# A two-layer trunk on one core: layer 0's twice-used weights kept in parts, one more parked MLP unit, and five smaller edits

## The chip, the cores and the metric

The kernel runs on one core of a Trainium2 chip. The metric is the device time of one execution in microseconds (us). Before the change it is 2128.24 us, the median of three executions (2126.32 to 2133.12).

Five engines work side by side, each through its own instructions in order: TensorE (PE, its weight loads shown as PEld), VectorE (DVE), ScalarE (ACT), GpSimd (POOL) and SyncE (SP, which here only issues transfers). POOL issues transfers too. An engine whose next instruction waits holds everything behind it.

## The reference

A stream `x` of 1024 positions by 1024 features passes two layers. Layer 0 mixes positions with a gated linear recurrence (RG-LRU), layer 1 with forgetting attention (FoX); beside it, each layer has four heads of cross-attention into 256 memory tokens. Then come an output projection and an MLP.

```python
def reference(x, mem, norm_mix, norm_mem, w_mem_kv, xa_q_gain, xa_k_gain, w_out,
              norm_mlp, w_mlp_in, w_mlp_out, w_in_a, conv_w, conv_b, ...):
    for layer in range(DEPTH):
        h = rms_norm(x, norm_mix[layer])
        j = layer // N_MIXERS
        if layer % N_MIXERS == 0:
            y_mix, xq = rglru_group(h, w_in_a[j], conv_w[j], conv_b[j], ...)
        else:
            y_mix, xq = fox_group(h, w_in_b[j], b_forget[j], fox_q_gain[j], fox_k_gain[j])
        y_mem = memory_group(xq, mem, norm_mem[layer], w_mem_kv[layer], ...)
        x = x + jnp.concatenate([y_mix, y_mem], axis=-1) @ w_out[layer]
        x = x + sqrelu_mlp(rms_norm(x, norm_mlp[layer]), w_mlp_in[layer], w_mlp_out[layer])
    return x

def sqrelu_mlp(h, w1, w2):
    return jnp.square(jax.nn.relu(h @ w1)) @ w2
```

## The kernel before, in words

**Products in parts.** Every fp32 operand is held as two fp32r parts: `hi` is a rounded copy (ACT) and `lo` the rest (a DVE subtraction). A product of one 128x128 block with 512 columns is three matmuls: hi·hi, hi·lo, lo·hi. The two halves of the sequence (512 positions each) are worked on apart; `h` is the half.

**Weights.** A plan lists the weights in the order of use, each entry 128 x 1024 (for the output projections 128 x 512). SP loads the raw entry into a ring of three buffers `wr`; `_wpart` writes the parts into rings of three: `wh` by ACT (L312) and `wl` by DVE (L313). One full entry feeds 24 matmuls of 512 columns, a half entry 12. `share()` (L263) holds a list of weight names: an entry of a listed name is, at its first use, also stored to HBM in its two parts (`wsp`, two stores on SP's queue), and at a later use both parts are loaded from there (L328, two transfers on POOL's queue, straight into the rings), with no raw load and no work of ACT and DVE. Before the change the list holds only layer 1's weights. In layer 0 `wina` (8 entries), `wxqa` (4) and `wout0` (8) are used by half 0 and again by half 1, and are loaded raw and parted both times.

**Statistics of a norm.** The squares of 8 tiles of 512 positions are summed either by adds on DVE and POOL into one tile (`sqacc`, L440) which one small product reduces (L374), or on PE: `sq_pe`/`sq_mm` (L443 to L457) multiply each square (as weights) with a one-column vector, four matmuls of 128x1 per tile, 32 per half; each of these fp32 matmuls is two records of the trace. `norm_split_first` (L517) starts the program: it loads and parts half 0 of `x`, then takes the statistics with `sqacc`.

**The MLP.** For each of 8 units (`g`) `mlp_z` makes a block of the hidden layer for both halves and `mlp_out` multiplies it with the second weight, both by a scheme of seven products in place of eight, named b11, b21, t2, t3, t1, t4, b22. `t1` to `t4` are sums of the two halves' inputs, parted by ACT (L468) and DVE (L471). A product over a full entry is 24 matmuls (`product`, L1004). DVE adds a product to a tile in `plus` (L1027); `relu2` is L1031 (DVE) and L1032 (ACT). Partial sums go to HBM by accumulating transfers on POOL's queue (`xspill`, L1161). In the last unit (g = 7) the residual is added by transfers too: four per block, accumulating `xs` into the tile `dst` (L1180).

**Parked units.** The products b11 and b21 of a unit need only half 0. `mlp_park` runs them early, as PE work that fills gaps. TUNE["park"] = (0, 1): these two units' products run inside layer 1's FoX attention, which `weave` interleaves with the other work by a rate. TUNE["wait"] = (2,): this unit's two products run after the last output projection (`outproj(1, K_X)`), ahead of the MLP loop. When a parked unit comes up in `mlp_z`, its kept result is put back into PSUM by a matmul with the identity (L1092), and t2 accumulates onto it.

**FoX.** Per head: scores on PE (L1396, mask L1398), a maximum on DVE (L1401), exponentials on ACT (L246), a scaling on POOL (L1413), transposes on PE (L1438), copies of the result by ACT and DVE (L1441, L1442), and products with the values on PE (L1428, L1429).

**Order.** The code is written in program order with generators; a scheduler of the language, by its own model of times, then sets the order on each engine. Line numbers after the change are higher: L381 becomes L385, L440 L444, L456 L462, L1011 L1017, L1092 L1103, L1396 L1413, L1413 L1430, L1428 L1445, L1429 L1446, L1438 L1455, L328 L332, L852 L858, L863 L869.

## Time and profile before

| what | value |
|---|---|
| median of three executions | 2128.24 us (2126.32 to 2133.12) |
| the profiled execution | 2132.55 us |
| its span, first to last instruction | 2130.8 us |
| outside the span | 1.75 us |
| busy: PE, DVE, ACT, POOL | 97%, 78%, 53%, 40% |
| mean granted TensorE clock | 0.989 |
| moved over HBM | 295.29 MB, 139 GB/s |

How to read the views: a window row gives, for a stretch of the span, its length and for PE, PEld, DVE, ACT, POOL the busy time with the number of records, then the granted clock (1.00 is full), the share of time in which the 16 DMA engines were busy, and GB/s. A row of groups gives line, engine, operation, output and input tiles, shapes, count, busy us, mean ns, and the idle time of the engine just before such instructions. A row of the timeline gives start, length, and in brackets the idle time before and what ended it. Matmul records overlap and their ends are modelled, so PE can lose time while it counts as busy.

The stages in the profiled execution, roughly: 0 to 220 us half 0 of layer 0's input projections and the memory group, 220 to 320 the same for half 1 with the recurrence and the output projection, then layer 0's MLP to about 950, the inputs of layer 1 to 1110, FoX woven with projections and parked units to 1467, the last output projection to 1503, and layer 1's MLP to the end.

### The profile page before, as it was taken

To read this page: it belongs to the slowest core of one execution; us is meant where nothing else is said; L and a number is where in the kernel's file an instruction comes from. 1 tells how busy PE (TensorE), PEld (TensorE's weight loads), DVE (VectorE), ACT (ScalarE), POOL (GpSimd) and SP (SyncE) were. 2 spreads that over 40 slices of the span, in tenths; PEclk is the share of its full clock that TensorE was granted. 3 is DMA by queue.
4 is the path that set the end of the run, shared out by engine and by line. 5 is a ranking of instruction groups with operands and counts; after the bars stand their busy time and mean duration, and the time that the engine had idled before them with its cause. 6 is when DMAs were issued, how large, how long until landed. Compare 5 with 4: busy or idle time off the path is not lost.

```text
span 2130.8 us, 29902 instructions
## 1 busy us (share of the span) xinstructions
PE 2065.7 (97%) x10402; PEld 1716.9 (81%) x10402; DVE 1654.5 (78%) x2712; ACT 1137.0 (53%) x2154; POOL 857.8 (40%) x847
## 2 busy tenths in 40 slices
PE   8999999999999999988999999999989999999999
PEld 6798878778778778767998998877767777787787
DVE  8987688886876877887686778776877778768867
ACT  6765645544444444465555647565544444544443
POOL 3222221434535535545332324422063544444444
PEclk9999999999999999999999999998999999999999
DMA  6323352446446545647767446844255574374375
GB/s 208 119 80 109 114 188 85 95 88 135 98 91 128 103 94 121 132 114 199 278 239 269 148 135 218 294 137 127 93 113 126 118 150 92 76 158 86 80 171 139
DMA packets 124952, 295.29 MB, mean 139 GB/s; under 512 B 14016, under 2 KB 16128, under 8 KB 124800
## 3 DMA queue, kind: packets, MB, share of 16 engines
q1 hardware_dynamic: 79872, 203.11, 28.4%
q0 software_dynamic: 44928, 90.26, 23.8%
q8 instruction: 82, 1.34, 0.3%
q14 instruction: 70, 0.57, 0.1%
HBM read 185.22 MB, written 108.10 MB: 138 GB/s over the span
## 4 chain that ended last, share of the span: by engine, by line
PE 55%; DVE 13%; issue 6%; DMA 4%; ACT 1%; POOL 1%; DVEq 0%; SPq 0%; POOLq 0%; ACTq 0%
PE pspt L1011 15%; PE pss L1011 12%; PE pspj L381 10%; PE pspj L1011 8%; DVE wl L313 3%; DVE r L471 3%; DVE f L1031 2%; DMA xspill<-f 2%; PE pso L1011 2%; PE pspt L381 1%; PE pspt L1438 1%; PE pss L1396 1%; DMA f<-xspill 1%; DVE f L1027 1%; DVE f L1130 1%
## 5 line engine op out<-in xcount | busy, mean ns | idle before, releaser
L313 DVE TENSOR_TENSOR wl<-wr,wh 128x1024 fp32r<-128x1024 f32 (+2 forms) x362 | 442.2, 1232 | 112.6 <-ACT wh L312 108.0
L1011 PE MATMUL pspt<-r,wh 128*128 128x512 f32 x1552 | 490.2, 396 | 8.0 <-DVE f L1027 6.1
L1161 POOL DMA_DIRECT2D xspill<-f x224 | 292.3, 2029 | 299.0 <-DVE f L1027 296.7
L312 ACT ACTIVATE wh<-wr 128x1024 fp32r<-128x1024 f32 (+3 forms) x411 | 305.8, 766 | 149.7 <-PE pss L1011 36.3
L1011 PEld LDWEIGHTS pspt<-r,wh 128*128 128x128 f32 x1552 | 291.3, 188 | 79.9 <-ACT r L468 4.6
L1011 PE MATMUL pss<-r,wh 128*128 128x512 f32 x1024 | 329.9, 401 | 13.9 <-DVE r L471 5.1
L1011 PE MATMUL pspt<-r,wl 128*128 128x512 f32 x776 | 307.4, 396 | 0.4 <-DVE wl L313 0.2
L471 DVE TENSOR_TENSOR r<-f,r 128x512 fp32r<-128x512 f32 x282 | 225.0, 808 | 100.3 <-DMA xspill<-f 57.6
L1011 PE MATMUL pspj<-r,wh 128*128 128x512 f32 x816 | 259.3, 397 | 4.1 <-ACT f L1022 1.8
L381 PE MATMUL pspj<-wh,r 128*128 128x256 f32 (+1 forms) x1280 | 246.7, 286 | 3.9 <-ACT wh L312 1.7
L1011 PEld LDWEIGHTS pss<-r,wh 128*128 128x128 f32 x1024 | 193.2, 189 | 70.0 <-DVE r L471 12.8
L468 ACT ACTIVATE r<-f 128x512 fp32r<-128x512 f32 x282 | 172.8, 626 | 115.7 <-DMA xspill<-f 50.6
L1032 ACT ACTIVATE f<-f 128x512 f32<-128x512 f32 x128 | 80.9, 632 | 268.0 <-DVE f L1031 267.7
L381 PEld LDWEIGHTS pspj<-wh,r 128*128 128x128 f32 x1280 | 200.9, 188 | 7.0 <-ACT wh L312 1.9
L351 POOL TENSOR_TENSOR wr<-wr,wr 128x512 f32<-128x512 f32 x60 | 94.6, 1777 | 271.6 <-DVE wl L313 258.8
L1011 PE MATMUL pss<-r,wl 128*128 128x512 f32 x512 | 203.7, 398 | 0.0
L1011 PEld LDWEIGHTS pspj<-r,wh 128*128 128x128 f32 x816 | 153.0, 188 | 41.5 <-ACT f L1022 2.3
L381 PE MATMUL pspj<-wl,r 128*128 128x256 f32 (+1 forms) x640 | 181.5, 284 | 1.2 <-DVE wl L313 1.1
L1011 PEld LDWEIGHTS pspt<-r,wl 128*128 128x128 f32 x776 | 147.2, 190 | 37.3 <-DVE wl L313 2.1
L381 PE MATMUL pspj<-r,wh 128*128 128x512 f32 x488 | 163.7, 411 | 9.6 <-ACT wh L312 5.9
L1011 PE MATMUL pspj<-r,wl 128*128 128x512 f32 x408 | 160.0, 397 | 0.4 <-DVE wl L313 0.4
L353 POOL TENSOR_TENSOR wr<-wr,f 128x512 f32<-128x512 f32 x60 | 140.2, 2650 | 17.8 <-issue 17.6
(297 smaller groups left out, 4012.2 us busy)
## 6 DMA issues: line engine op xcount, KB each, us to landing
wr<-in_w_dram SPq DMA_DIRECT2D x134, 512.0 KB, 4.4
xspill<-f POOLq DMA_DIRECT2D x224, 256.0 KB, 6.8
f<-xspill SPq DMA_DIRECT2D x80, 256.0 KB, 3.9
xspill<-f SPq DMA_DIRECT2D x64, 256.0 KB, 3.8
f<-in_xT_dram SPq DMA_DIRECT2D x32, 256.0 KB, 3.4
wr<-in_wkv_dram SPq DMA_DIRECT2D x16, 512.0 KB, 4.0
wr<-in_wina_dram SPq DMA_DIRECT2D x15, 512.0 KB, 3.5
wsp<-wh SPq DMA_DIRECT2D x14, 512.0 KB, 4.7
```

The source lines that it names most:

```text
L312: self.wact = self.nc.scalar.activation(hi, raw, AF.Copy)
L313: eng.tensor_tensor(lo, raw, hi.bitcast(F32), ALU.subtract)
L351: G.tensor_tensor(r["a11"][:, d], r["a11"][:, d], r["a21"][:, d], ALU.subtract)
L353: G.tensor_tensor(r["a12"][:, d], r["a12"][:, d], x, ALU.subtract)
L381: self.lastmm = self.nc.tensor.matmul(out, lhsT=a, rhs=b, start=(j == 0), stop=(j == n - 1))
L468: i = self.nc.scalar.activation(hi[:, :n], src, AF.Copy)
L471: self.nc.vector.tensor_tensor(lo[:, :n], src, hi[:, :n].bitcast(F32), ALU.subtract)
L1011: self.lastmm = self.nc.tensor.matmul(ps, lhsT=a, rhs=b, start=(start and c == 0 and j == 0), stop=(c == n - 1 and j == 2), skip_group_che ...
L1027: self.nc.vector.tensor_tensor(f[:, :H], f[:, :H], ps, ALU.add)
L1031: self.nc.vector.scalar_tensor_tensor(f[:, n], src, 0.0, self.rsb[h][:, n], ALU.max, ALU.mult)
L1032: self.lastsq = self.nc.scalar.activation(f[:, n], f[:, n], AF.Square)
L1161: nc.gpsimd.dma_start(self.xs[2 * q + a, :, b * H:(b + 1) * H], f[:, n], accum_op=ALU.add)
```

## The change

1. Eight matmuls of 128 columns of ones are put at PE's start, before any data.
2. `wina`, `wxqa` and `wout0` join the list in `share()`: 20 entries of 512 KB per part are stored at first use (40 stores on SP) and loaded in parts at the second use (12 full entries of 2 x 512 KB and 16 half entries of 2 x 256 KB on POOL's queue).
3. `norm_split_first` uses `sq_pe`: eight adds (four on DVE) become 32 matmuls of 128x1, 64 records.
4. Unit 2 moves from "wait" to "park". Unit 3 becomes "wait": its b11 product runs before `outproj(1, K_X)`, its b21 after it.
5. For parked units other than 0, ACT copies the kept result into PSUM in place of the identity matmul.
6. In g = 7 of both layers, the block (0, 0) gets its residual by four POOL additions from tiles that SP loads at t1, in place of four accumulating transfers.

```diff
@@ TUNE
-    "park": (0, 1),
-    "wait": (2,),
+    "park": (0, 1, 2),
+    "wait": (3,),
@@ Builder.__init__
+        warm = self.psum("pt")
+        for _ in range(8):
+            nc.tensor.matmul(warm[:, :P], lhsT=self.ones, rhs=self.ones, start=True, stop=True)
@@ share
-            if len(e) < 5 or e[3][0] not in ('wkb','wqb','wvb0','wvb1','wxqb','wout1m','wout1x'):
+            if len(e) < 5 or e[3][0] not in ('wina','wxqa','wout0','wkb','wqb','wvb0','wvb1','wxqb','wout1m','wout1x'):
@@ sq_pe (and norm_split_first calls it)
-    def sq_pe(self, m, h, xt):
+    def sq_pe(self, m, h, xt, behind=None):
         sq = self.F.get()
-        self.nc.scalar.activation(sq[:, :H], xt, AF.Square)
+        i = self.nc.scalar.activation(sq[:, :H], xt, AF.Square)
+        if behind is not None:
+            self.after(i, behind)
...
-            self.sqacc(k, h, xt[k][:, :H], self.nc.vector if k % 2 else self.nc.gpsimd, last)
+            self.sq_pe(k, h, xt[k][:, :H], last)
@@ plan_mlp and the plan of layer 1
         for g in wait:
-            self.plan_unit("w1", 8 * l + g, Unit.ALL[:2])
+            self.plan_unit("w1", 8 * l + g, Unit.ALL[1:2])
...
+        for g in TUNE["wait"]:
+            self.plan_unit("w1", 8 + g, Unit.ALL[:1])
         self.plan += [self.ent("wout1x", m, 512, 1) for m in range(8)]
@@ mlp_park
         yield from self.product([self.psum("pj") for _ in range(2)], b11, True, self.copies(t))
         kept = []
+        if pause:
+            yield None
@@ mlp_z
-                nc.tensor.matmul(A[o], lhsT=self.ident, rhs=t[o][:, n], start=True, stop=True)
+                if g:
+                    nc.scalar.activation(A[o], t[o][:, n], AF.Copy)
+                else:
+                    nc.tensor.matmul(A[o], lhsT=self.ident, rhs=t[o][:, n], start=True, stop=True)
@@ mlp_out
-                if g == 7:
+                if g == 7 and a == b == 0:
+                    f = self.acc.pop(0)
+                    G.tensor_tensor(dst[q][:, n], dst[q][:, n], f[:, n], ALU.add)
+                    self.F.put(f)
+                elif g == 7:
                     nc.gpsimd.dma_start(dst[q][:, n], self.xs[2 * q + a, :, b * H:(b + 1) * H], accum_op=ALU.add)
@@ the end of the FoX stage
+        wait = [self.mlp_park(g, True) for g in TUNE["wait"]]
+        for p in wait:
+            while next(p) is not None:
+                pass
         drain(self.outproj(1, K_X, self.xs, self.xs, "gmlp1", True, ("pj", "s", "pt")))
         self.pool_parts = TUNE["pm1"]
-        self.mlp(1, TUNE["wait"])
+        self.mlp(1, wait)
```

The order on the engines moves at three places. First PE near the end of FoX, at the scores of one of the last heads (`pss` takes scores and, at L381, products of the output projection; `pso` the sums over values, `pspj` products of parked units). Before:

```order
L1396 MATMUL pss_14769<-r_1459_14148,r_1456_14134 128x512
L1396 MATMUL pss_14769<-r_1459_14148,r_1457_14135 128x512
L1398 MATMUL pss_14769<-msk,idr 128x128
L381 MATMUL pss_14986<-r_1356_13394,wh_73 128x512
L381 MATMUL pss_14986<-r_1357_13395,wh_73 128x512
L381 MATMUL pss_14986<-r_1356_13394,wl_76 128x512
```

After:

```order
L1413 MATMUL pss_14585<-r_1151_11370,r_1458_14194 128x512
L1413 MATMUL pss_14585<-r_1151_11370,r_1459_14195 128x512
L1017 MATMUL pspj_15060<-r_1503_14504,wh_73 128x512
L1017 MATMUL pspj_15060<-r_1504_14505,wh_73 128x512
L1017 MATMUL pspj_15060<-r_1503_14504,wl_76 128x512
L1017 MATMUL pspj_15060<-r_1515_14558,wh_73 128x512
L1445 MATMUL pso_14410<-r_1499_14476,r_1046_10501 128x512
L1017 MATMUL pspj_15060<-r_1516_14559,wh_73 128x512
L1017 MATMUL pspj_15060<-r_1515_14558,wl_76 128x512
L1017 MATMUL pspj_15060<-r_1521_14570,wh_73 128x512
L1017 MATMUL pspj_15060<-r_1522_14571,wh_73 128x512
L1446 MATMUL pso_14410<-r_1500_14477,r_1046_10501 128x512
```

The 72 matmuls of unit 2's two products and of unit 3's first (L1017) now stand between the rows of the attention's last heads; before, the only other work there was some of the output projection (L381).

Second, POOL in layer 0 during half 1's recurrence (L858 and L869 are scalar steps of the recurrence's scan, L444 adds of squares, the transfers are the new part loads of `wout0`). Before, POOL had these there, and no transfers:

```order
L852 TENSOR_SCALAR f_284_2866<-f_284_2866 128x512
L852 TENSOR_SCALAR f_283_2864<-f_283_2864 128x512
L440 TENSOR_TENSOR f_271_2797<-f_271_2797,f_293_2985 128x512
L863 TENSOR_SCALAR f_281_2860<-f_281_2860 128x512
L863 TENSOR_SCALAR f_282_2862<-f_282_2862 128x512
```

After:

```order
L869 TENSOR_SCALAR f_281_2926<-f_281_2926 128x512
L869 TENSOR_SCALAR f_282_2928<-f_282_2928 128x512
L332 DMA wh_74<-wsp_124 128x512
L332 DMA wl_77<-wsp_125 128x512
L869 TENSOR_SCALAR f_284_2932<-f_284_2932 128x512
L444 TENSOR_TENSOR f_271_2861<-f_271_2861,f_303_3111 128x512
L869 TENSOR_SCALAR f_283_2930<-f_283_2930 128x512
L332 DMA wh_73<-wsp_128 128x512
L332 DMA wl_76<-wsp_129 128x512
```

The loads of a part pair stand behind steps of the scan, which wait for DVE; two pairs (into buffers 74/77 and 73/76) are held that way, and the later ones follow one another.

Third, PE between the last output projection and the MLP of layer 1 (L456 and L462 are the norm's statistics). Before:

```order
L1011 MATMUL pspj_15254<-r_1514_14498,wh_74 128x512
L1011 MATMUL pspj_15254<-r_1515_14499,wh_74 128x512
L1011 MATMUL pspj_15254<-r_1514_14498,wl_77 128x512
L456 MATMUL pso_14978<-cD,f_1611_15172 128x1 x4
L456 MATMUL pso_14978<-cD,f_1614_15200 128x1 x4
L1011 MATMUL pss_15409<-r_1620_15221,wh_74 128x512
```

After:

```order
L1017 MATMUL pspt_15479<-r_1630_15398,wh_75 128x512
L462 MATMUL pso_15152<-cD,f_1626_15384 128x1 x4
L1017 MATMUL pspt_15478<-r_1631_15399,wh_75 128x512
L1017 MATMUL pspt_15478<-r_1630_15398,wl_78 128x512
L1017 MATMUL pspt_15479<-r_1631_15399,wh_75 128x512
L1017 MATMUL pspt_15479<-r_1630_15398,wl_78 128x512
L1017 MATMUL pss_15550<-r_1632_15405,wh_73 128x512
```

Before, a waiting unit's product stood ahead of the last statistics and t3 (`pss`) right behind them. Now t2 of unit 0 (`pspt`) stands ahead of them and four of its matmuls behind them, then t3.

More of the change, by code (lines that the diff above doesn't have):

```diff
@@ L86, in __init__ @@
         self.need = {n: () for n in names}
-        if "a11" in pos:
-            self.need["a11"], self.need["a12"] = ("a11",), ("a12",)
+        for k in ("a11", "a12"):
+            if k in pos:
+                self.need[k] = (k,)
         if full:
@@ L1013, in product @@
                 if c % 2 and c + 1 < n:
-                    yield
+                    yield 1
             if done is not None:
                 done(o, ps)
-            yield
+            yield 1
     def copies(self, dst):
@@ L1032, in relu2, with mlp_park @@
         self.lastsq = self.nc.scalar.activation(f[:, n], f[:, n], AF.Square)
-    def mlp_park(self, g):
+    def mlp_park(self, g, pause=False):
         t = []
@@ L1223, in hook7 @@
                 advance(nxt)
-        for g in wait:
+            if key == "t1":
+                self.acc = [self.load_x(2 * q, 0, self.xs) for q in range(4)]
+        for p in wait:
             for k in ("t3", "t1"):
                 self.xsplit(k)
-            drain(self.mlp_park(g))
+            drain(p)
         for g in range(8):
@@ L1668, in run @@
             self.R.put(v)
+        wait = [self.mlp_park(g, True) for g in TUNE["wait"]]
+        for p in wait:
+            while next(p) is not None:
+                pass
         drain(self.outproj(1, K_X, self.xs, self.xs, "gmlp1", True, ("pj", "s", "pt")))
         self.pool_parts = TUNE["pm1"]
-        self.mlp(1, TUNE["wait"])
+        self.mlp(1, wait)
 @with_exitstack
```

## The prediction

> **What bounds the kernel now.** I read the page first, then windows over the stages, then the waits and the timeline where a window loses time. The page:
>
> ```profile
> span 2130.8 us, 29902 instructions
> PE 2065.7 (97%) x10402; PEld 1716.9 (81%) x10402; DVE 1654.5 (78%) x2712; ACT 1137.0 (53%) x2154; POOL 857.8 (40%) x847
> ```
>
> PE is recorded busy for 97% of the span, so the kernel is bound by the count of matmuls plus the places where PE stands still or runs slowly. Work taken from DVE or ACT is worth something only at such a place. The windows, with the engines in the order of the header:
>
> ```profile
> core 0: us, PE busy (x) PEld busy (x) DVE busy (x) ACT busy (x) POOL busy (x), PEclk, DMA share, GB/s
> 5.40:13.60 8.20, 7.33 (x16) 4.95 (x17) 7.33 (x23) 6.88 (x13) 0.00 (x0) 1.00 1.02 367
> 30.60:34.10 3.50, 3.50 (x11) 2.87 (x11) 3.50 (x12) 0.00 (x0) 0.00 (x0) 0.51 0.33 112
> 280.00:400.00 120.00, 116.24 (x523) 93.22 (x522) 105.45 (x161) 68.83 (x112) 25.77 (x22) 0.99 0.42 125
> 286.65:290.06 3.41, 3.31 (x8) 2.63 (x9) 3.41 (x6) 2.26 (x5) 0.00 (x0) 0.50 1.00 368
> 1333.00:1361.00 28.00, 27.17 (x142) 22.19 (x141) 23.03 (x61) 16.11 (x41) 17.70 (x26) 1.00 1.04 352
> 1390.00:1467.00 77.00, 70.36 (x378) 55.65 (x378) 57.69 (x160) 50.30 (x121) 23.77 (x40) 1.00 0.36 103
> 1467.60:1481.30 13.70, 13.70 (x46) 11.44 (x46) 6.57 (x10) 5.25 (x9) 4.03 (x8) 0.50 0.68 212
> 1505.20:1512.00 6.80, 5.07 (x11) 3.57 (x12) 6.80 (x16) 2.52 (x4) 0.00 (x0) 0.50 0.01 2
> 1516.00:1590.00 74.00, 68.81 (x289) 53.56 (x288) 54.01 (x60) 34.62 (x56) 30.16 (x25) 1.00 0.38 102
> ```
>
> Two kinds of loss show: idle time (77.00 − 70.36 = 6.64 us in 1390 to 1467), and stretches at half the clock, which follow an idle time and cost half their busy time. The idle times that the change touches, from the timeline:
>
> ```profile
> 29.70 1.05 PE L374 MATMUL pso<-cD,f 128*128 128x1 f32 x8 [2.70 <-DVE f L440]
> 286.75 0.80 PE L924 MATMUL pspt<-r,wl 128*128 128x512 f32 x1 [2.46 <-DVE wl L313]
> 951.62 0.77 PE L1011 MATMUL pspt<-r,wh 128*128 128x512 f32 x1 [4.18 <-DVE f L1027]
> 1506.15 1.22 PE L1011 MATMUL pss<-r,wh 128*128 128x512 f32 x2 [2.35 <-ACT r L468]
> 1508.15 0.79 PE L1011 MATMUL pss<-r,wh 128*128 128x512 f32 x1 [0.79 <-DVE r L471]
> ```
>
> The pace of PE where nothing holds it, for scale, is this piece of the chain that ended last: 24 matmuls of 512 columns, one product, in 5.58 us, 0.233 each.
>
> ```profile
> 1592.02 5.58 PE pspt L1011 x24
> ```
>
> The profiled execution took 2132.55 us, its span plus 1.75 outside it, and is 4.31 above the median of the runs, 2128.24. I sum against the profiled one and give the difference on the median. About 0.3%, 6.4 us, is what a measurement here can tell from no change.
>
> **Part by part.**
>
> Warm-up matmuls. They have no input to wait for and stand before the first data. PE's first product waits for loads: in 5.40 to 13.60 the DMA engines are busy all the time (1.02), and 16 records there take 7.33 us where 16 × 0.233 would take 3.73. If the pace there were set by the clock, up to 7.33 − 3.73 = 3.6 us would be won. I take 0: PE then stands idle again until the first loads land, and 2.46 us of idle before 286.75 were enough to bring the half clock of 286.65 to 290.06. Range −3.6 to 0.
>
> Statistics on PE at the start. The price of one record is from the same operation further on, 16 in 1.84 us:
>
> ```profile
> 1501.96 1.84 PE L456 MATMUL pso<-cD,f 128*128 128x1 f32 x16
> ```
>
> 64 records × 0.115 = +7.4. The eight records at 29.70 go (−1.05), with their wait (−2.70) and the half clock behind it (3.50 × 0.5 = −1.75). That is +1.9, of which PE's idle time in 5.40 to 13.60 (8.20 − 7.33 = 0.87) can hold some: I take **+1**. Range: −5.5 if all of the new records lie beside waits for loads, +6.4 if none does and the idle time only moves. What the adds free on DVE is no gain, since PE isn't waiting for DVE elsewhere in that stage.
>
> Layer 0's second half in parts. The work that goes from DVE and ACT, by these groups of 280 to 400:
>
> ```profile
> L313 DVE TENSOR_TENSOR wl<-wr,wh 128x1024 fp32r<-128x1024 f32 x10 | 12.2, 1223 | 3.5 <-ACT wh L312 3.4
> L312 ACT ACTIVATE wh<-wr 128x1024 fp32r<-128x1024 f32 x10 | 10.6, 1056 | 6.3 <-PE pspt L1011 2.7 <-PE pspj L1011 2.6 <-DMA wr<-in_w_dram 0.9
> L313 DVE TENSOR_TENSOR wl<-wr,wh 128x512 fp32r<-128x512 f32 x14 | 9.6, 682 | 0.3 <-ACT wh L312 0.3
> ```
>
> DVE loses 12 × 1.22 + 16 × 0.68 = 25.5 us of work, ACT 12 × 1.06 and the half entries. Almost all of it lies beside PE's work; the one wait that it makes is 286.75, where `wl` stood behind the scan on DVE: −2.46, and the half clock 3.31 × 0.5 = −1.7, together −4.2. What comes instead is the latency of the part loads. For layer 1's entries, which already go this way:
>
> ```profile
> L328 POOL DMA_DIRECT2D wh<-wsp x32: 527/548/647, 1151.7 to 1483.9; - x32
> DMA to landing us min/median/max: 2.6/5.3/9.6
> wh<-wsp POOLq DMA_DIRECT2D x16, 256.0 KB, 3.9
> wl<-wsp POOLq DMA_DIRECT2D x16, 256.0 KB, 4.8
> ```
>
> A half entry feeds 12 matmuls, 12 × 0.233 = 2.8 us. In a ring of three the period is the larger of 2.8 and (L + 2.8)/3, L from the buffer's release to the landing; it stays 2.8 up to L = 5.6. The 256 KB loads took 3.9 and 4.8 (mean 4.35), so the steady run is covered by the two other buffers. Two pairs can't be issued early, since POOL stands at steps of the scan before them; with one buffer's work as cover each shows 4.35 − 2.8 = 1.55, together +3. Sum **−1.2**, range −4.2 to +8. The 20 MB of stores go out in the first half; SP's later raw loads stand behind them, but a store waits for the same subtraction that frees the raw buffer.
>
> Layer junction, g = 7. The four accumulating transfers become POOL additions. A POOL addition took
>
> ```profile
> L351 POOL TENSOR_TENSOR wr<-wr,wr 128x512 f32<-128x512 f32 x60 | 94.6, 1777 | 271.6 <-DVE wl L313 258.8
> 949.67 1.21 DVE L313 TENSOR_TENSOR wl<-wr,wh 128x1024 fp32r<-128x1024 f32 x1
> 950.80 0.67 DVE L1027 TENSOR_TENSOR f<-f,pspt 128x512 f32<-128x512 f32 x1
> ```
>
> 1.78 us, against a transfer of some us. The wait of 4.18 at 951.62 ended with the DVE addition of 950.80, which stood behind the weight subtraction of 949.67; in the new order the addition comes ahead of it. So −1.2, with the POOL additions free where POOL has time (40% busy). But POOL's additions slow DVE:
>
> ```profile
> L1031 DVE SCALAR_TENSOR_TENSOR f<-f,f 128x512 f32<-128x512 f32 x6 | 8.0, 1352 | 0.0
> L1031 DVE SCALAR_TENSOR_TENSOR f<-f,f 128x512 f32<-128x512 f32 x4 | 2.7, 684 | 0.0
> ```
>
> The same operation took 1352 ns on average in 280 to 400 and 684 in 1390 to 1467. I take 0.2 for that: **−1**, range −5 (the whole wait and more) to +3 (four DVE operations at +0.67).
> [...]
>
> FoX tail. Three products more, 3 × 5.58 = 16.8 us of PE work, now stand among the last heads' rows, and leave the MLP stage. In 1390 to 1467 PE was idle for 6.64; the waits are short and many, which is what a filler covers. DVE is 57.69 of 77.00 busy, 75%; the three products add to it three weight subtractions and four operations of 512, 3 × 1.22 + 4 × 0.68 = 6.4 us, and about as much to ACT. I take the whole idle and nothing of the time in which a busy PE loses pace: **−6.6**. Range 0 (each filler is paid for by DVE and ACT being later) to −6.64 − 6.85 = −13.5, if the half clock of 1467.60 to 1481.30 (13.70 × 0.5) goes as well.
> [...]
>
> After the last output projection. Before, 3.14 us of idle (2.35 + 0.79) stood between the statistics and t3, and a half clock with 5.07 × 0.5 = 2.5. Now t2 of unit 0 is there as filler, but only four of its matmuls (0.93 us) stand behind the last statistics: t3's parts are late by DVE and ACT as before. I take 0.93 of the idle and some 1.1 of the clock: **−2**. Range −5.6 (all) to +5.2 (the idle of 1516 to 1590, 74.00 − 68.81, once more, because unit 2's products no longer lie there).
>
> Identity matmuls.
>
> ```profile
> 1484.26 1.72 PE pspt L1092 x4
> L1441 ACT ACTIVATE r<-pspt 128x512 fp32r<-128x512 f32 x22 | 12.2, 592 | 4.6 <-PE pso L1428 2.4 <-PE pspt L1438 2.0
> ```
>
> Each record took 0.43 on PE; units 1, 2 and now 3 need none, so eight of twelve go: **−3.4**. ACT copies six tiles, 0.59 each by the row of L1441, 53% busy. If t2 had to wait for each pair, it would be 3 × 1.2 = 3.5 us, and the term 0.
>
> Sum: 0 + 1 − 1.2 − 1 − 6.6 − 2 − 3.4 = −13.2, so 2119.35 for an execution like the profiled one, and 2128.24 − 13.2 = **2115.0** on the median. The ends of the terms are extremes. As independent errors they give the root of the squares, 12 below and 15 above; two thirds of it is my forecast's own range, 2107 to 2125.
>
> **Rivals.**
>
> *All gaps filled.* The filler also removes the half clock at 1467.60 and all of the idle after the output projection: the FoX term −13.5 and the next −5.6, together −13.2 − 6.9 − 3.6 = −23.7, 2104.5; with a warm-up that works 2101. For it: DVE is only 75% busy in the tail, POOL 31%. Against: the half clock began at the end of the tail, behind a chain of the last head that no earlier filler shortens.
>
> *The tail is a chain of latencies.* Scores, maximum, exponentials, transposes and copies of the last heads set the end; three products' DVE and ACT work lengthens it as much as PE gains, and t3 waits as before. FoX and the next term are 0: −13.2 + 6.6 + 2 = −4.6, 2123.6, within 0.3%. For it: the order has t3 right behind the statistics still. That the warm-up does nothing belongs here as in my forecast.
>
> *Part loads late (slower).* In layer 0 the loads share the DMA engines with SP's loads and are issued by POOL behind the scan. At L = 9.6, the longest landing of the row, the half entries' period is (9.6 + 2.8)/3 = 4.13, 16 × 1.33 = 21.3 more, and the two pairs show 2 × 6.8 = 13.6: the term is −4.2 + 34.9 = +30.7, and the total −13.2 + 31.9 = +18.7, 2146.9. It decides from L = 7.0 on (7.33 × L − 35.5 = 13.2 + 3), and by 0.3% from L = 7.9. For it: such landings exist, in 1333 to 1361, where the DMA share is 1.04. Against: in 280 to 400 the share is 0.42, and loads of 512 KB in place of 256 KB of raw add less than as much again.
>
> **How the numbers follow.** My forecast 0.5, all gaps filled 0.18, the chain of latencies 0.2, part loads late 0.12. Below 2121.8 (faster by over 0.3%) lie nearly all of the first (0.47), all of the second and a quarter of the third (0.05): 0.70. Above 2134.6 lies most of the last (0.10) and little else (0.01): 0.11. Between: 0.19. The range goes from 2099, under the best case by the same two thirds of its unknown terms, to 2131, above the chain of latencies with its statistics term at the upper end; outside it stay most of the late loads and a few per cent below.
>
> **What would show it.** In the new trace: (1) no idle time at 29.70 and 64 more records of 128x1 before 45 us; (2) no wait for `wl` near 286, and waits of layer 0's second half for `wh<-wsp` and `wl<-wsp` of under 5 us in all; (3) in the last 77 us of FoX an idle time of PE under 2 us, and the stage itself longer by about 10 (16.8 − 6.6), with MLP shorter by 16.8; (4) behind the last statistics about 2 us of idle before t3; (5) four records of the identity matmul. Landings over 7 us in 220 to 400, or an FoX stage longer by the full 16.8, would make it wrong; so would waits of t2 for ACT's copies.

## The result

The changed kernel takes 2149.21 us (median of four runs, 2146.76 to 2152.37), beside 2129.47 of the kernel before on the same chip: a ratio of 1.0090, 95% interval 1.0073 to 1.0106. It is slower by 19 us where I forecast a gain of 13. The profiled execution took 2148.11 us, 15.6 more than the one of before, so the profile shows most of the loss.

The page of the changed kernel, its first two lines:

```profile
span 2146.4 us, 30066 instructions
PE 2077.2 (97%) x10466; PEld 1733.0 (81%) x10466; DVE 1628.6 (76%) x2668; ACT 1122.7 (52%) x2120; POOL 885.2 (41%) x900
```

PE is busy for 97% as before, with 64 records more: 64 of statistics and 16 of warm-up come, 8 of the old statistics and 8 of identity matmuls go. DVE has 26 us less to do (1654.5 to 1628.6), as the sum had it, and the kernel is slower all the same. Where the time went is read from the MLP's accumulating transfers, 112 per layer, whose line has its first and last start in a row (L1161 before, L1172 after):

```profile
L1161 POOL DMA_DIRECT2D xspill<-f x224: 846/1690/4885, 391.4 to 2055.5; - x112
```

```profile
L1172 POOL DMA_DIRECT2D xspill<-f x224: 853/1718/4912, 399.5 to 2066.8; - x112
```

The first is 8.1 us later, the last 11.3, and the end of the span 15.6: half of the loss is made before layer 0's MLP, 3.2 between there and the last transfer of layer 1, 4.3 in the last unit. Each of these positions is of one execution. Four kernels that share the code up to the first of these transfers (this one, and those without part 6, without part 4 and with the later fetch below) have it at 399.5, 399.6, 403.2 and 401.1, so a shift of under 4 us in one pair of profiles shows nothing by itself. The windows of the changed kernel that answer to those of before:

```profile
core 0: us, PE busy (x) PEld busy (x) DVE busy (x) ACT busy (x) POOL busy (x), PEclk, DMA share, GB/s
13.25:23.49 10.24, 10.24 (x62) 8.91 (x61) 7.41 (x22) 8.88 (x16) 0.00 (x0) 1.00 1.04 405
23.49:37.15 13.66, 13.66 (x50) 12.21 (x50) 11.06 (x28) 7.45 (x18) 4.51 (x4) 0.50 0.88 343
132.72:136.13 3.41, 3.03 (x14) 3.03 (x15) 2.64 (x14) 0.34 (x2) 1.85 (x5) 0.50 0.18 65
1390.00:1467.00 77.00, 74.91 (x390) 61.95 (x389) 58.21 (x150) 50.16 (x111) 20.68 (x35) 0.98 0.47 151
1733.57:1740.40 6.83, 6.08 (x14) 4.79 (x15) 5.13 (x5) 6.73 (x12) 2.96 (x2) 0.50 0.14 19
2112.45:2115.86 3.41, 3.36 (x9) 2.15 (x8) 3.41 (x5) 1.81 (x4) 1.37 (x1) 0.50 0.00 0
```

The half clock stands out. The row of before for the start had 3.50 us at 0.51; now it is 13.66 us at 0.50, and PE never stands still in them. The mean clock of the execution falls from 0.989 to 0.983:

```profile
core 0: 2146.4 us, clock 0.983
```

The windows of all stretches at half clock, added up, before (six stretches) and after (twelve):

```profile
sum 44.37, PE 38.99 PEld 31.92 DVE 36.90 ACT 22.13 POOL 13.23; mean PE 6.50 PEld 5.32 DVE 6.15 ACT 3.69 POOL 2.21
```

```profile
sum 75.10, PE 65.59 PEld 54.05 DVE 63.71 ACT 43.26 POOL 30.62; mean PE 5.47 PEld 4.50 DVE 5.31 ACT 3.60 POOL 2.55
```

PE is busy for 26.6 us more at half pace, which is 13.3 us of work lost. Of the 15.6 us that the span grew, 11.5 are busy time of PE (2065.7 to 2077.2) and 4.1 idle time (65.1 to 69.2), so the slower pace is about the size of the first part. So the theories to test were what brings each of these stretches, and which waits stand ahead of them. Three waits of the changed kernel, from its timeline:

```profile
133.10 0.58 PE L385 MATMUL pspj<-wh,r 128*128 128x256 f32 x1 [4.03 <-DMA wh<-wsp]
1734.32 1.22 PE L1017 MATMUL pss<-r,wh 128*128 128x512 f32 x2 [2.91 <-ACT f L1028]
2111.78 0.50 PE L1017 MATMUL pss<-r,wh 128*128 128x512 f32 x1 [3.05 <-DVE r L477]
```

The first belongs to part 2 (a part load), the second to part 4 (unit 2 in the MLP), the third to part 6 (POOL's additions in the last unit).

### The profile page after: what moved, and what is told of

Same layout as the page of the kernel before. It is cut to its first block, busy times and chain, and to the rows that moved or that the text cites. A ratio compares the mean times of both kernels' runs of the same rounds, so it can differ in the third digit from the quotient of the medians.

```text
span 2146.4 us, 30066 instructions
## 1 busy us (share of the span) xinstructions
PE 2077.2 (97%) x10466; PEld 1733.0 (81%) x10466; DVE 1628.6 (76%) x2668; ACT 1122.7 (52%) x2120; POOL 885.2 (41%) x900
## 4 chain that ended last, share of the span: by engine, by line
PE 35%; DVE 8%; DMA 4%; issue 4%; ACT 2%; POOL 1%; SPq 0%; DVEq 0%; POOLq 0%; ACTq 0%
PE pspj L385 9%; PE pspt L1017 7%; PE pss L1017 6%; PE pspj L1017 5%; DVE r L477 2%; DVE wl L317 1%; DMA xspill<-f 1%; DMA f<-xspill 1%; PE pss L1413 1%; DVE f L1037 1%; PE pspt L385 1%; PE pspt L1455 1%; DMA f<-cscr 1%; PE pso L1017 1%; DVE f L1033 1%
## 5 line engine op out<-in xcount | busy, mean ns | idle before, releaser
L1017 PE MATMUL pspt<-r,wh 128*128 128x512 f32 x1536 | 485.2, 396 | 8.1 <-DVE r L477 2.6
L317 DVE TENSOR_TENSOR wl<-wr,wh 128x1024 fp32r<-128x1024 f32 (+3 forms) x322 | 400.2, 1252 | 117.6 <-ACT wh L316 111.9
L1172 POOL DMA_DIRECT2D xspill<-f x224 | 292.5, 2097 | 286.8 <-DVE f L1033 283.4
L316 ACT ACTIVATE wh<-wr 128x1024 fp32r<-128x1024 f32 (+3 forms) x371 | 282.0, 782 | 151.3 <-DMA wr<-in_w_dram 45.5
L1017 PE MATMUL pss<-r,wh 128*128 128x512 f32 x1024 | 333.9, 404 | 23.2 <-ACT f L1028 12.0
L1017 PEld LDWEIGHTS pspt<-r,wh 128*128 128x128 f32 x1536 | 288.0, 188 | 79.5 <-DVE r L477 4.2
L477 DVE TENSOR_TENSOR r<-f,r 128x512 fp32r<-128x512 f32 x282 | 235.7, 847 | 100.8 <-ACT r L474 47.8
L1017 PE MATMUL pspt<-r,wl 128*128 128x512 f32 x768 | 304.8, 397 | 0.5 <-DVE wl L317 0.4
L1017 PE MATMUL pspj<-r,wh 128*128 128x512 f32 x832 | 265.7, 400 | 2.1 <-DVE f L1033 1.0
L1017 PEld LDWEIGHTS pss<-r,wh 128*128 128x128 f32 x1024 | 194.4, 191 | 80.8 <-DVE r L477 14.2
L1017 PE MATMUL pss<-r,wl 128*128 128x512 f32 x512 | 204.9, 401 | 0.0
L1017 PEld LDWEIGHTS pspj<-r,wh 128*128 128x128 f32 x832 | 156.6, 190 | 39.4 <-ACT f L1028 1.3
L1017 PEld LDWEIGHTS pspt<-r,wl 128*128 128x128 f32 x768 | 145.7, 190 | 36.8 <-DVE wl L317 2.2
L385 PE MATMUL pspj<-r,wh 128*128 128x512 f32 x488 | 164.4, 410 | 6.4 <-ACT r L474 2.1
L1017 PE MATMUL pspj<-r,wl 128*128 128x512 f32 x416 | 162.8, 397 | 0.0
```

Of the source, the lines that this page charges most:

```text
L316: self.wact = self.nc.scalar.activation(hi, raw, AF.Copy)
L317: eng.tensor_tensor(lo, raw, hi.bitcast(F32), ALU.subtract)
L385: self.lastmm = self.nc.tensor.matmul(out, lhsT=a, rhs=b, start=(j == 0), stop=(j == n - 1))
L477: self.nc.vector.tensor_tensor(lo[:, :n], src, hi[:, :n].bitcast(F32), ALU.subtract)
L1017: self.lastmm = self.nc.tensor.matmul(ps, lhsT=a, rhs=b, start=(start and c == 0 and j == 0), stop=(c == n - 1 and j == 2), skip_group_che ...
L1172: nc.gpsimd.dma_start(self.xs[2 * q + a, :, b * H:(b + 1) * H], f[:, n], accum_op=ALU.add)
```

## The experiments

Theory A: the loss is a sum of such waits and half clocks, one or two for each of parts 2, 3, 4 and 6. Its first rival, B: late part loads in layer 0 carry it alone, as my slower case had it. C and D deny A's reading of parts 4 and 3; E and F, later, are on what brings the half clock. Ratios are to the kernel before on the same chip in the same runs; the changed kernel stands at 1.0090.

**Part 6 undone.**

```diff
-                if g == 7 and a == b == 0:
-                    f = self.acc.pop(0)
-                    G.tensor_tensor(dst[q][:, n], dst[q][:, n], f[:, n], ALU.add)
-                    self.F.put(f)
-                elif g == 7:
+                if g == 7:
...
-            if key == "t1":
-                self.acc = [self.load_x(2 * q, 0, self.xs) for q in range(4)]
```

> The changed kernel with part 6 undone: the residual of block (0, 0) comes by four accumulating transfers again. Theory A (the loss is a sum of small terms; POOL's additions block DVE): in the changed kernel's last unit three POOL additions of 5.09 us stand beside three DVE operations of 1.77 in place of 0.68, then PE waits 3.05 us and runs at half clock; so the last unit is shorter by about 4 us and the junction of the layers by 2 to 3: about -6.5 against the changed kernel, +13 against the kernel before. Theory B (late part loads in layer 0 alone): no difference, +19 against the kernel before.

Measured: 1.0036 (1.0023 to 1.0049), −0.54%. In the profile the first accumulating transfer is as late as with the change and the end of the span 7.8 earlier: 3.3 by the last transfer of layer 1, 4.5 in the last unit. The mechanism is in the changed kernel's timeline, POOL first, then DVE:

```profile
2105.49 5.09 POOL L1192 TENSOR_TENSOR f<-f,f 128x512 f32<-128x512 f32 x3 [2.99 <-ACT f L1028]
```

```profile
2105.38 0.68 DVE L1147 TENSOR_TENSOR f<-f,f 128x512 f32<-128x512 f32 x1
2105.98 1.77 DVE L477 TENSOR_TENSOR r<-f,r 128x512 fp32r<-128x512 f32 x1
2107.68 1.77 DVE L1138 TENSOR_TENSOR f<-f,f 128x512 f32<-128x512 f32 x1
2109.38 1.75 DVE L1149 TENSOR_TENSOR f<-f,f 128x512 f32<-128x512 f32 x1
2111.05 1.28 DVE L477 TENSOR_TENSOR r<-f,r 128x512 fp32r<-128x512 f32 x2
```

From 2105.49 to 2110.6 POOL adds, and in just this time three DVE operations take 1.77 us in place of 0.68: 3.3 us late. The fourth, behind them, is what PE waits for at 2111.78, and the half clock of 3.41 follows. Without part 6 the waits of that stretch are gone:

```profile
PE pss L1017 <- ACT r L474: 0.7, 1, 0.7
```

At the junction of the layers the changed kernel shows the same, POOL first:

```profile
947.10 6.30 POOL L1192 TENSOR_TENSOR f<-f,f 128x512 f32<-128x512 f32 x4 [0.70 <-ACT f L1028]
948.83 1.75 DVE L477 TENSOR_TENSOR r<-f,r 128x512 fp32r<-128x512 f32 x1
950.63 0.50 PE L1017 MATMUL pspt<-r,wh 128*128 128x512 f32 x1 [2.57 <-DVE r L477]
956.47 1.22 PE L1017 MATMUL pss<-r,wh 128*128 128x512 f32 x2 [2.29 <-ACT r L474]
```

Three DVE operations in a row, from 948.83 to 953.9, take 1.75 to 1.77 us. Without part 6 the two waits are 0.48 and 0.49, but the old one of 4.18 is back at 4.17, where the change has 2.08. Layer 0's last spill store (L1177) starts at 1007.0 with the change and at 1003.6 without part 6, 3.4 earlier.

Theory A's mechanism holds, with a size of 0.54% against its 0.3. The undoing also takes out SP's four loads at t1 and their tiles, so the time is that of the part as a whole; that DVE's slowness beside POOL carries it is read from the two timelines. Theory B, no difference, falls: the intervals do not meet.

**Part 4 undone.** Park (0, 1), wait (2), with the plan and the calls as before the change.

```diff
-    "park": (0, 1, 2),
-    "wait": (3,),
+    "park": (0, 1),
+    "wait": (2,),
```

> The changed kernel with part 4 undone: units 0 and 1 are parked in FoX, unit 2 waits until after the last output projection. Theory A (a third unit fetched from HBM costs tiles): the waits of t2's bank for ACT's copies at the end of the b21 product of mlp_out for units 1 and 2 (3.03 and 2.91 us, each with a half clock behind it) are smaller, -9, but the filling of FoX (+4 us of use) is lost: about -5 against the changed kernel. Theory C (the filler is what helps and the stalls come from elsewhere): +4 against the changed kernel. Theory B: no difference.

Measured: 1.0064 (1.0044 to 1.0085), −0.26%. It points to theory A, and theory C's +4 lies outside; but the interval overlaps the changed kernel's (1.0073 to 1.0106), so that part 4 costs anything is not shown by this run alone.

**Part 2 undone.**

```diff
-'wina','wxqa','wout0','wkb','wqb',
+'wkb','wqb',
```

> The changed kernel with part 2 undone: layer 0's second uses are loaded raw and parted by ACT and DVE again. Theory A: the wait of 4.03 us for a part load at 133 us and its half clock go, the one behind the scan's DVE work stays: -3 to -6 against the changed kernel. Theory B (late part loads carry the whole loss): -18 or so, level with the kernel before or better.

Measured: 1.0008 (0.9995 to 1.0021), −0.82%: by the time it is what theory B expects, which part 6 has already ruled out as the whole. Nor does its profile put the loss in layer 0 alone:

```profile
L1172 POOL DMA_DIRECT2D xspill<-f x224: 845/1662/4865, 393.7 to 2056.0; - x112
```

The first transfer is 5.8 us earlier than with the change, the last 10.8. In the first 400 us no wait above 1.3 us is left: the one at 133 is gone, and so is one of 3.34 at 281. The rest is in layer 1. From 1500 to 1800 PE's waits for ACT's copies (L1028) are 8.2 us in place of 12.0, and the half clock from 1510 to 1800 is 3.4 us in place of 17.1. This can't be put down to part 2 as it stands: with the sums by 512-column matmuls, an edit at the start (below), the same waits fall to 7.0.

**Part 3 undone.**

```diff
-            self.sq_pe(k, h, xt[k][:, :H], last)
+            self.sqacc(k, h, xt[k][:, :H], self.nc.vector if k % 2 else self.nc.gpsimd, last)
```

> The changed kernel with part 3 undone: the first norm's squares are added on DVE and POOL again. Theory A: 64 records at 0.11 us go, of which the old wait of 2.7 us and its half clock come back: -2 to -4 against the changed kernel. Theory D (statistics on PE hide in the time in which PE waits for loads): +2 to +4. Theory B: no difference.

Measured: 1.0065 (1.0042 to 1.0088), −0.25%. Theory D's +2 to +4 lies outside the interval; that of theory A overlaps the changed kernel's, as with part 4. The same stretches as above:

```profile
13.25:23.49 10.24, 10.24 (x41) 8.18 (x41) 9.93 (x24) 7.84 (x14) 2.60 (x3) 0.90 1.03 388
23.49:37.15 13.66, 13.66 (x75) 11.67 (x74) 13.47 (x27) 9.82 (x24) 7.84 (x4) 1.00 0.93 352
```

The second has the full clock; the 0.90 of the first is the end of another half clock, from 8.50 to 15.33. The end of this profile is no earlier (2146.5), since other half clocks stand in it at 93.83, 145.03 and 278.15. All six profiles with `sq_pe` at the start have 13.65 us at half clock, one of them 17.07, from 22 to 25 us on; none without it has.

**Part loads on SP.**

```diff
-                    nc.gpsimd.dma_start(b, d[:, a:a + n])
+                    (nc.sync if k[0] in ('wina', 'wxqa', 'wout0') else nc.gpsimd).dma_start(b.bitcast(F32), d[:, a:a + n].bitcast(F32))
```

> The changed kernel with layer 0's part loads issued by SP in place of POOL. Theory A1 (the loads at 126 us are late because POOL issues them behind the scan's last step, which waits for DVE): the wait of 4.03 us at 133 us and its half clock go, so that layer 0 ends about 5 us earlier: -4 to -6 against the changed kernel. Theory A2 (the loads are late because the transfers themselves are slow beside the stores): the wait stays, 0 against the changed kernel.

Measured: 1.0052 (1.0034 to 1.0071), −0.38%; the wait is down to 0.80, at 130.86, with no half clock behind it, and the first accumulating transfer is 4.6 earlier:

```profile
L1172 POOL DMA_DIRECT2D xspill<-f x224: 842/1694/4880, 394.9 to 2061.9; - x112
```

Theory A1. POOL's timeline of the changed kernel shows how it came:

```profile
120.02 1.46 POOL L869 TENSOR_SCALAR f<-f 128x512 f32<-128x512 f32 x1 [3.97 <-DVE f L868]
124.75 1.47 POOL L869 TENSOR_SCALAR f<-f 128x512 f32<-128x512 f32 x1 [3.28 <-DVE f L868]
126.17 0.56 POOL L332 DMA_DIRECT2D wl<-wsp  x1
126.74 0.54 POOL L332 DMA_DIRECT2D wh<-wsp  x1
```

The two loads go out the moment that POOL is through with the scan's step, for which it waited on DVE, and land at 130.3 and 133.1. At 133.10 PE goes on, after 4.03 us. The second took 6.3 us to land, where the median of these loads is 4.8, so about 1.5 us is the transfer's and the rest its late issue.

**The fetch of the parked tiles, later.**

```diff
         yield from run([self.psum(k) for k in more], "b21", True, c11[1], "t3")
-        mid()
         yield from run(A, "t2", False, c21[0], "t1")
...
         yield from run(A, "t1", False, c22[1], "b22")
+        mid()
```

> The changed kernel with the fetch of the next parked unit's four tiles moved from behind the product b21 to behind t1 in mlp_out. Theory A (tiles): ACT's copies of t2's result wait for tiles that the accumulating transfers have not yet left, because the fetch took four tiles just before; so the waits at 1576, 1662 and 1734 us (6.09, 3.03, 2.91) fall under 1 each and their half clocks go with them: -10 to -16 against the changed kernel. Theory C (ACT is simply late with its copies): no change, -1 to +1.

Measured: 1.0085 (1.0061 to 1.0109), no difference. The waits changed name. With the change, from 1500 to 1800 us:

```profile
PE pss L1017 <- ACT f L1028: 12.0, 3, 6.1
```

With the later fetch:

```profile
PE pspt L1017 <- DVE f L1033: 8.1, 2, 7.8
PE pspt L1017 <- ACT pspt L1101: 3.7, 2, 1.9
```

The waits for tiles of units 1 and 2 go, as theory A has it, but the fetched tiles then come late, and t2 waits for part 5's copies (L1101). Unit 0's wait only moves. So scarce tiles are a part of it, and moving the fetch is no cure.

**Part 5 alone on the kernel before.** The four lines of the diff in `mlp_z`; the change's generators for the waiting units are there too, and do nothing here.

> The kernel before with part 5 alone: ACT copies the kept tiles of units 1 and 2 into PSUM in place of identity matmuls. Both theories: four fp32 matmuls of 512 columns go, eight records at 0.43 us each: -3.4 against the kernel before if t2 never waits for the copies; 0 if it waits about 1.2 us for each of the pairs.

Measured: 0.9996 (0.9980 to 1.0012). Its one profile ends 8 us earlier, its ten times do not: the 3.4 us are inside the interval and not shown.

**Parts 1, 4 and 5 with the later fetch.** The edits above together (2, 3 and 6 undone, `mid()` moved).

> Parts 1, 4 and 5 alone (2, 3 and 6 undone), with the late fetch. Theory A: part 4 now wins what the idle of FoX's tail holds, -4 to -8, part 5 -3, and the waits for tiles that the kernel before has too (2.31, 1.53, 1.18, 1.16, 1.02 in 1557 to 1647 us) mostly go: -10 to -16 against the kernel before. Theory C: -3 to -7.

Measured: 1.0015 (0.9997 to 1.0033). Both theories were too hopeful. That FoX's filling pays for itself is not shown.

**Sums by 512-column matmuls.** This is the test of the half clock at the start: the same PE time, other shapes.

```diff
-            self.sq_pe(k, h, xt[k][:, :H], last)
+            sq = self.F.get()
+            self.after(self.nc.scalar.activation(sq[:, :H], xt[k][:, :H], AF.Square), last)
+            if k == 0:
+                ps = self.psum("o")
+            self.nc.tensor.matmul(ps, lhsT=self.ident, rhs=sq[:, :H], start=k == 0, stop=k == 7)
...
```

ACT's copy of the sum out of the bank, which follows, is left out here.

> The changed kernel, but the first norm's squares are summed on PE by eight matmuls of 512 columns with the identity as weights (accumulated in one bank, copied out by ACT, then reduced by the four small matmuls of the kernel before), in place of 32 matmuls of one column. The PE time of both is about the same at full clock (16 records of 0.43 and 8 of 0.11, 7.8 us, against 64 of 0.11, 7.4). Theory E (the stretch of 13.65 us at half clock from 23 to 37 us comes from the one-column matmuls, which keep the array busy by record and nearly empty): the stretch shrinks to 3.4 or 6.8, so -3.5 to -5 in layer 0. Theory F (the half clock comes from PE's waits before it): it stays at 13.65, 0 to +1.

Measured: 1.0032 (1.0016 to 1.0047), −0.58%. Its groups from 20 to 45 us hold the new matmuls, and its windows show the clock:

```profile
L540 PE MATMUL pso<-f,ident 128*128 128x512 f32 x16 | 7.4, 592 | 0.0
```

```profile
13.25:23.49 10.24, 10.24 (x37) 7.53 (x37) 7.42 (x22) 7.93 (x15) 0.00 (x0) 0.90 1.02 401
23.49:37.15 13.66, 13.66 (x54) 9.39 (x53) 9.93 (x25) 10.36 (x24) 3.90 (x3) 1.00 0.93 359
```

The stretch at half clock is gone entirely, with PE busy by record for all of it in both kernels. This is theory E's case: what counted here was not that PE was busy, but with what. The groups of the changed kernel in 23.49 to 37.15 show what was there:

```profile
L462 PE MATMUL pso<-cD,f 128*128 128x1 f32 x34 | 7.2, 343 | 0.0
L385 PE MATMUL pss<-r,wh 128*128 128x512 f32 x8 | 4.2, 628 | 0.0
```

Over half of the busy time (7.2 of 13.66) are matmuls of one column. The weight loads are nearly the same in both (50 and 53 records), so they are not the difference. The end of the stretch fits too. It ends four times 3.41 us after its start, 3.41 being the shortest stretch at half clock in this profile, and its quarters end at 26.90, 30.32, 33.73 and 37.15. The last one-column matmuls stand here:

```profile
29.29 3.41 PE L462 MATMUL pso<-cD,f 128*128 128x1 f32 x16
```

They end at 32.70, in the third quarter; the fourth is the first without any, and the full clock follows it. With part 4 undone they end at 33.53, inside the quarter from 32.72 on, and there the stretch has one more (17.07). A few of them did not bring it: in the kernel with 512-column sums eight records of one column (0.95 us, at 33.52) stand between wide matmuls at a clock of 1.00.

The time is more than theory E's −3.5 to −5: −0.58% is 12 us. The first accumulating transfer comes 4.9 us earlier than with the change, the end of layer 0 6.1 (its last spill store, 1000.9 against 1007.0), the end of the span 13.1. What lies behind layer 0 is not shown to be this edit's.

**The same at another place: the last norm of layer 1 off PE, on the kernel before.**

```diff
-                (self.sqacc if gain is None else self.sq_pe)(m, h, xv)
+                self.sqacc(m, h, xv, nc.vector if gain is not None and m > 5 else None)
```

> The kernel before, with the statistics of layer 1's last norm (half 1, L456 in the last output projection) taken off PE: the eight squares are added by POOL (six) and DVE (two). Theory E (one-column matmuls bring the half clock): the 13.65 us at half clock at 1468 shrink to 3.4 or 6.8, -3.5 to -5, and 64 records at 0.115 go, of which eight stay: -6.4; -8 to -11 against the kernel before, if no wait for the later sum shows. Theory F (the half clock comes from the wait of 2.06 us before it): the dip stays, -3 to -6.

Measured: 0.9970 (0.9958 to 0.9982), −6.4 us by the ratio, faster than the kernel before. The 13.7 us at half clock at 1467 become twice 3.4, as theory E says, the first behind the same wait of 2.06 us as before, the second behind waits of 1.61 and 0.74 for part loads; but the later sum makes two waits, and a new half clock of 10.2 us stands there (timeline and window of this kernel):

```profile
1499.75 1.02 PE L374 MATMUL pso<-cD,f 128*128 128x1 f32 x8 [3.81 <-DVE f L440]
1505.74 0.79 PE L1011 MATMUL pss<-r,wh 128*128 128x512 f32 x1 [3.92 <-DVE r L471]
```

```profile
1466.54:1469.96 3.42, 3.42 (x9) 2.52 (x9) 1.51 (x3) 0.39 (x1) 1.33 (x3) 0.50 0.04 16
1469.96:1481.31 11.35, 9.00 (x30) 6.49 (x29) 11.18 (x12) 6.79 (x12) 8.18 (x10) 0.85 0.95 286
1500.68:1510.92 10.24, 6.32 (x15) 4.54 (x16) 10.24 (x21) 3.12 (x5) 0.00 (x0) 0.50 0.07 26
```

That is why −6.4 came and not −8 to −11. The mean clock over its twelve executions is 0.988, and that of the kernel before 0.988 too: the half clock moved and did not shrink in all, and −6.4 is about the price of the 56 records that went (56 × 0.115 = 6.4). The time fits theory F's −3 to −6 nearly as well; for E speaks the row of the clock at this place, which F wanted unchanged at 13.7.

**That and part 5.** Both edits on the kernel before.

> The same with part 5 of the change (ACT copies in place of identity matmuls): another -3.4 if the copies are free, so -11 to -14 against the kernel before by theory E, -6 to -9 by theory F.

Measured: 0.9962 (0.9949 to 0.9975). It is the fastest of all kernels here; against the one without part 5 (0.9970) the intervals overlap. By the ratio it is 8 us, less than theory E's 11 to 14 and inside theory F's 6 to 9; the half clock of 10.2 us stands in its profile too, at 1504.72.

**Part 1 alone on the kernel before.** Only the eight warm-up matmuls.

> The kernel before with the eight warm-up matmuls alone. Theories E and F alike: PE is idle again until the first loads land, and the first product is bound by loads, so -1 to +1 by the end of layer 0's first recurrence, and no difference of the time.

Measured: 1.0006 (0.9992 to 1.0021). No difference in the time, as expected. Its one profile is not as expected: the first accumulating transfer is at 399.2, 7.8 later than before where −1 to +1 was forecast, with half clocks at 79.83 (3.41) and 100.31 (10.24) that the kernel before has not. The four profiles without part 1 have this transfer at 391.4 to 392.9. The kernel of parts 1, 4 and 5 has it at 396.5; the three kernels that follow, with part 1 in them and parts 2 and 3 mended, at 393.4 to 394.5. So the eight matmuls may have a share in the 8.1 us ahead of layer 0's MLP; the interval leaves room for up to 4.5 us (0.0021 × 2130), and this stays open.

**Three mended at once.** Part loads on SP, sums by 512-column matmuls, part 6 undone.

> The changed kernel with three parts mended at once: layer 0's part loads on SP, the first norm's squares summed by eight matmuls of 512 columns, the residual by transfers as before. If the three causes are independent, their single effects on the ratio (0.38, 0.58 and 0.54%) add to 1.5% and this is 0.6% faster than the kernel before, -13. If they share the same half clocks and waits, the sum is less: the profiles put layer 0's loads at 5, the first norm at 5 and part 6 at 7.4, together 17, so about level with the kernel before, -3 to +1.

Measured: 1.0003 (0.9988 to 1.0018): level with the kernel before, so the causes overlap, and mending the three takes away the whole loss. The clock of its profile is above that of the kernel before (0.989), the mean over its executions hardly (0.988 against 0.987):

```profile
core 0: 2131.9 us, clock 0.992
```

**The same without part 4.**

> The same with part 4 undone as well. If part 4 costs in MLP (a third unit's tiles and copies, +5.5) what it wins in FoX (-4 to -8), this is the same within 3. If part 4 is a loss, as the single undo hinted, this is about 5 faster; if it is a gain once the rest is mended, 3 to 5 slower.

Measured: 0.9983 (0.9973 to 0.9992), the only kernel made from the changed one that is faster than the kernel before, by 3.6 us. Against the one with part 4 it is 0.20%, some 4 us, though the two intervals just overlap (0.9988 to 0.9992). This and the single undo (0.26%) point the same way: part 4 costs about 4 us. PE's waits from 1500 to 1800 for ACT's copies, with part 4 and without:

```profile
PE pss L1023 <- ACT f L1034: 9.0, 4, 6.1
```

```profile
PE pss L1023 <- ACT f L1034: 4.8, 3, 2.3
```

**The three mended, and the last norm off PE.** The edit of the kernel before on top of the first of these.

> The first of these with the last norm's squares off PE too. Theory E (dense one-column matmuls bring the half clock at the start of the last output projection): the half clock at 1490 to 1505 shrinks and 6.4 us of records go: -4 to -8 against the first of these, as the same edit gave -6.4 on the kernel before.

Measured: 0.9995 (0.9978 to 1.0012), −0.08% where −0.2 to −0.4 was expected. The edit doesn't repeat its gain here; with the squares off PE, PE stands idle for 5.75 us from 1490 to 1540 where the kernel without this edit has 1.92, and the clock of that stretch is 0.83 against 0.93. Two waits stand there, 2.63 for a part load and 2.08 for a DVE addition of the output projection (L907).

## Why the prediction was wrong

**Statistics at the start: the step that failed most plainly.** "64 records × 0.115 = +7.4 ... I take **+1**". The price of a record came from a place where the clock was full and 16 one-column records in a row stood behind a product of 24 wide ones, 1.84 us for the 16. At the start 42 stand in one row (20.72, 6.43 us) and 16 in another; there the clock is down to half, and the row of 16 took 3.41, nearly twice as long. The wide ones between them are slowed too (`pss<-r,wh` 628 ns each by record, 407 from 37.1 to 60). The sum removed a half clock of 3.5 us behind the old wait, but the change put one of 13.66 in its place: 10.2 × 0.5 = 5.1 us, and with it the term is about +6 in place of +1. Undoing the part gave −0.25%, 5.3 us; mending the shapes alone gave −0.58%, more than the term. The row that could have warned stood in the prediction: 1467.60 to 1481.30, 13.70 us at 0.50 with PE busy for all of it. I counted it as a half clock that an idle time had brought and did not ask what PE was busy with.

**Layer 0 in parts.** That loads stand on POOL behind the scan was in my term. But I placed it in half 1's scan only and priced two pairs at 1.55 each. The first second uses (`wxqa`) lie behind half 0's scan, from 113 us on; a pair issued at 126 was late, PE waited 4.03 and lost 1.5 more (3.03 × 0.5) at half clock. And of the expected −4.2 nothing came, since another wait for a subtraction took the old one's place:

```profile
281.52 0.50 PE L385 MATMUL pss<-r,wl 128*128 128x512 f32 x1 [3.34 <-DVE wl L317]
```

The landings of all transfers of the parts in the changed kernel:

```profile
DMA to landing us min/median/max: 2.6/4.9/9.0
```

So the transfers as a whole were not slow (5.3 median before, 9.6 the longest), and the price was mainly the time of issue. The term is +5 to +6 in layer 0 by the profiles, not −1.2. Undoing the part gave −0.82%, more than that; where the rest comes from, in layer 1, is not settled. That the slower rival's 2146.9 lies near the 2149.2 measured is luck: it had +31 for slow landings at all half entries, and nothing like it is in the trace.

**Junction.** "I take 0.2 for that: **−1**". Undone, the part gives back 3.4 us at the junction and 4.5 in the last unit, 7.8 in all by the end of the span. The second I had left out: the part changes g = 7 of both layers, and I priced one. The first alone is past my range's upper end of +3; I had taken the middle. DVE's 1.77 against 0.68 was in my rows (1352 against 684 on average), and it makes three operations late by 3.3 us where I allowed 0.2. The three start within the 5.09 us of POOL's additions; at the junction, too, the three of 1.75 to 1.77 start within POOL's 6.30 us from 947.10. Why DVE is slower beside them is not shown.

**FoX and behind it.** In 1390 to 1467 PE's idle time fell from 6.64 to 2.09, and no wait stands before t3, so this half of the reasons held. But one half clock of 3.41 us is new there, at 1412.72, and the parked unit must come back: in the MLP its tiles are fetched from HBM, and ACT's copies wait for tiles that the accumulating transfers have not yet released:

```profile
1733.67 0.60 ACT L1028 ACTIVATE f<-pss 128x512 f32<-128x512 f32 x1 [5.24 <-DMA xspill<-f]
```

PE then waited 2.91 us at 1734, and 6.83 us at half clock began: some 6 us that no term had. By the two undos (0.26 and 0.20%, with intervals that overlap) the part costs 4 to 5 us where two terms gave −8.6. That the tiles are the cause is in part argued: the later fetch moved the waits and did not end them.

**Identity matmuls and warm-up.** Eight records went, as counted, but −3.4 is not shown by the times (0.9996). The warm-up won nothing, as forecast. My row from 5.40 to 13.60 reads a clock of 1.00, but the wide matmuls in it were as slow as at half clock: three took 1.28 us (9.72 to 11.00), as three at 0.50 did (32.44 to 33.72). In the changed kernel the row reads 0.50 from 9.84 to 13.25, so the eight matmuls did not bring the full pace.

**The forecast's build.** Every term was a balance of durations at full clock, with the half clock counted only where it would go, and put at nothing where it would come. The terms that came out wrong share this: 26.6 us more of PE's busy time at half pace are 13.3 us, beside a loss of 15.6. In the sum's own terms the misses are about 5 us (statistics), 6 to 7 (layer 0), 9 (junction), 13 (FoX and behind it, the largest) and 3 (identity), 36 to 37 together; measured were 19.7 + 13.2 = 33 us past the forecast. The add-up is rough, since the causes overlap.

## What to carry to other kernels

Price a small matmul by the clock around it: here packed one-column matmuls, 7.2 of 13.66 us, kept PE busy by record at a clock of 0.50, and the same sum by wide matmuls, 7.4 us, left it at 1.00. A load waits for the engine that issues it (behind POOL's scan PE waited 4.03 us for one, with the loads on SP 0.80), so give loads to a queue that does not wait for compute. In this kernel, additions moved from transfers to POOL were paid by DVE, three of whose operations took 1.75 to 1.77 us beside them in place of 0.68, and a unit parked early had to be fetched again late.

## What the runs showed of the hardware

- A granted clock of 0.50 for 13.66 us with PE busy by record throughout, when over half of that time (7.2 us) were 128x1 matmuls; with 16 records of 128x512 in their place (0.59 us each by record) the clock was 1.00 in the same stretch. The 13.66 us are four lengths of 3.41, PE was busy by record in all four, and the clock came back only after the first of them without one-column matmuls (33.73 to 37.15).
- Three DVE operations of 128x512 took 1.77, 1.77 and 1.75 us beside POOL additions of 1.70 each, 0.68 without.
- Half-clock stretches came in lengths near 3.41 us and its multiples: 3.41 (two), 6.83 (two), 10.24 and 13.65 in the kernel before, 3.41 (six), 6.83 (four) and 13.65 (two) in the changed one, and one of 17.07 without part 4.
